# A first stage in a written-out order on all engines, its norm row spread by TensorE, its first tokens and row requested from two queues

## The chip, the cores and the metric

One core of a Trainium2 chip runs the whole kernel. The metric is device time in microseconds, from the start of the program to its end, as the median of several executions. One execution was also taken by the profiler. TensorE is called PE here (its weight loads PEld), VectorE DVE, ScalarE ACT, GpSimd POOL and SyncE SP.

## What is computed

The reference is a trunk of two layers on 512 tokens of 1024 features, in float32. In each layer:

- h = x / rms(x) * g_pre, for each token over its 1024 features;
- proj = h @ w_in, cut into queries, keys, values, gates and the inputs of the two branches below;
- a sparse attention branch (compressed, selected and window keys) and a gated linear attention branch;
- y = m_nsa * (o_nsa @ w_up_nsa) + m_gla * (o_gla @ w_up_gla), and out = y @ w_out;
- x = x + rms_norm(out) * g_post.

The stage that the change rewrites is the start of the first layer: the norm of all tokens, the transposes that put features on partitions, and the first 296 columns of the projection (two groups of values, the attention gates and the 16 columns of the decay gate).

## The kernel before

Nearly all of the kernel's time goes to dense products on PE. To keep float32 accuracy, each operand of a projection is split in two: a high part H (a copy rounded to a shorter mantissa, made by ACT) and a low part Lo (the difference, made by DVE). One product of reference is three on PE: high by high, high by low, low by high (`split3`, L158).

**The first stage.** The tokens lie in four tiles s = 0 to 3 of 128 tokens, each loaded as two halves of 512 features (`load_x`, L218). `load_rows` (L186) asks for the norm row g_pre as two transfers that write the same 2 KB half row to all 128 partitions. `norm_rows` (L192) squares one half on ACT (L196) and one on DVE (L197), adds the sums, takes the power -1/2 on POOL (L183) and scales both halves by it and by the norm row on DVE (L202). `to_hT` (L205) transposes eight 128x128 blocks on PE (L209), copies each half out of PSUM as high part on ACT (L212) and makes the low part on DVE (L213). The weights of these 296 columns come in three pieces A0, A1, A2 (three, three and two blocks of 128 features), each loaded into one of three `raw` buffers (L132) and split by ACT (L145) and DVE or, for A1, POOL (L146). `proj_A(s)` (L314) runs 8 times 3 products of 296 columns for tile s, and half way through it the transposes of tile s+1. Its result is read out at L322 to L324. The stage so has 96 products and 32 transposes on PE.

**What follows.** `proj_gv` (L328) runs 24 products of 512 columns for each tile; its weights gv0 to gv3 pass through the same three `raw` buffers, so that gv3 can be requested only when gv0 has been split. gv1 and gv2 reuse the split buffers of A0 and A1. Small operands (`wa_s`, `gaT`, L361 to L369) are prepared on ACT and DVE in the same stretch. Then come long runs of projections (`fm`, L164), put out piece by piece by `fill` between the steps of the attention. There each pair of score blocks makes a round trip through DRAM (L783, L786), and PE multiplies what comes back (L841).

**Order.** PE's order is the program's (`manual_schedule` for PE, L224). The other engines' instructions are put in order by a planner that works with modelled costs. Each engine then runs its instructions strictly in that order, and so does the queue of SP, which issues every transfer. The constant masks are made on POOL and DVE (`masks`, L231), interleaved by the planner with the first stage.

## Time and profile before

| | us |
|---|---|
| median of 3 runs | 818.92 |
| lowest and highest run | 813.81, 818.93 |
| the profiled execution, whole | 817.14 |
| its span, first to last instruction | 815.1 |
| PE busy in the span | 787.2 (97%) |
| DVE busy | 553.8 (68%) |
| ACT busy | 353.5 (43%) |
| POOL busy | 99.9 (12%) |

The profiled execution lies 1.78 us below the median of the runs and 3.33 us above the lowest. What the profile does not show of it (817.14 less 815.1) is 2.04 us around the span. Times in the rows below count from the span's start. "Busy" is the time in which an engine had an instruction under way; matmuls are pipelined, so their durations overlap, and their rate is read from the distance of their starts.

### The profile page before, as it was taken

To read this page: it belongs to the slowest core of one execution; us is meant where nothing else is said; L and a number is where in the kernel's file an instruction comes from. 1 tells how busy PE (TensorE), PEld (TensorE's weight loads), DVE (VectorE), ACT (ScalarE), POOL (GpSimd) and SP (SyncE) were. 2 spreads that over 40 slices of the span, in tenths; PEclk is the share of its full clock that TensorE was granted. 3 is DMA by queue.
4 is the path that set the end of the run, shared out by engine and by line. 5 is a ranking of instruction groups with operands and counts; after the bars stand their busy time and mean duration, and the time that the engine had idled before them with its cause. 6 is when DMAs were issued, how large, how long until landed. Compare 5 with 4: busy or idle time off the path is not lost. (4 is left out here: it accounts for less than half of the span.)

```text
span 815.1 us, 12017 instructions
## 1 busy us (share of the span) xinstructions
PE 787.2 (97%) x4250; PEld 646.6 (79%) x4250; DVE 553.8 (68%) x1272; ACT 353.5 (43%) x727; POOL 99.9 (12%) x118
## 2 busy tenths in 40 slices
PE   3999999999989999999999999999999999999996
PEld 3888788888868787888888878888878788788885
DVE  5653848899987963655574457599999988266323
ACT  4591136555443533543246513456545544244211
POOL 3100024000000102121010101321000101022100
PEclk9999999999999999999999999999999999999999
DMA  8442124358486674556246112244666676655222
GB/s 296 140 147 78 52 59 137 95 175 247 154 245 208 191 235 127 171 157 218 78 143 220 53 52 79 78 116 129 211 201 217 209 231 200 192 155 157 77 104 77
DMA packets 54555, 124.55 MB, mean 153 GB/s; under 512 B 6592, under 2 KB 23520, under 8 KB 54496
## 3 DMA queue, kind: packets, MB, share of 16 engines
q1 hardware_dynamic: 54496, 123.79, 49.2%
q8 instruction: 33, 0.54, 0.3%
q14 instruction: 26, 0.21, 0.1%
HBM read 95.46 MB, written 25.17 MB: 148 GB/s over the span
## 5 line engine op out<-in xcount | busy, mean ns | idle before, releaser
L160 PE MATMUL ps_mm<-hT,hl 128*128 128x512 f32 x544 | 217.5, 400 | 0.0
L161 PE MATMUL ps_mm<-hT,hl 128*128 128x512 f32 x544 | 212.4, 390 | 0.0
L162 PE MATMUL ps_mm<-hT,hl 128*128 128x512 f32 x544 | 212.1, 390 | 0.0
L145 ACT CAST hl<-raw 128x1024 fp32r<-128x1024 f32 (+3 forms) x110 | 100.2, 913 | 147.0 <-PE ps_mm L161 102.2
L146 DVE TENSOR_TENSOR hl<-raw,hl 128x1024 fp32r<-128x1024 f32 (+3 forms) x109 | 119.2, 1095 | 51.2 <-ACT hl L145 46.0
L160 PEld LDWEIGHTS ps_mm<-hT,hl 128*128 128x128 f32 x544 | 102.3, 188 | 23.2 <-issue 3.1
L162 PEld LDWEIGHTS ps_mm<-hT,hl 128*128 128x128 f32 x544 | 102.2, 188 | 22.2
L161 PEld LDWEIGHTS ps_mm<-hT,hl 128*128 128x128 f32 x544 | 102.5, 188 | 19.0
L815 ACT ACTIVATE g<-g,sx 128x128 f32<-128x128 f32 (+3 forms) x128 | 70.9, 555 | 68.2 <-DVE sx L813 67.6
L778 DVE STREAM_TRANSPOSE T<-g 128x256 f32<-128x256 f32 (+3 forms) x128 | 58.6, 490 | 0.7
L818 DVE TENSOR_SCALAR g<-g,sx,gt 128x128 f32<-128x128 f32 (+3 forms) x128 | 57.1, 459 | 1.5
L161 PE MATMUL ps_mm<-oT,hl 128*128 128x512 f32 x128 | 50.5, 394 | 1.7 <-POOL oT L849 1.7
L160 PE MATMUL ps_mm<-oT,hl 128*128 128x512 f32 x128 | 51.2, 400 | 0.0
L162 PE MATMUL ps_mm<-oT,hl 128*128 128x512 f32 x128 | 50.1, 391 | 0.0
L841 PE MATMUL ps_o<-PT,a 128*64 128x256 f32 (+1 forms) x384 | 39.8, 353 | 4.6 <-DMA PT<-tp 4.6
L849 POOL TENSOR_TENSOR oT<-p,oT 128x512 fp32r<-128x512 f32 x8 | 13.9, 1738 | 241.7 <-ACT oT L848 241.7
L841 PEld LDWEIGHTS ps_o<-PT,a 128*64 128x64 f32 x384 | 26.1, 138 | 19.2 <-issue 10.2
L183 POOL TENSOR_TENSOR rs<-ms,mhalf 128x1 f32<-128x1 f32 (+1 forms) x24 | 18.0, 751 | 175.1 <-DVE ms L181 170.5
L869 POOL TENSOR_TENSOR p<-p,g 128x512 f32<-128x512 f32 x16 | 28.0, 1751 | 84.2 <-DVE p L868 78.5
L162 PE MATMUL ps_mm<-hl,hT 128*128 128x296 f32 (+1 forms) x96 | 32.7, 341 | 1.4 <-DVE hT L213 1.4
L160 PE MATMUL ps_mm<-hl,hT 128*128 128x296 f32 (+1 forms) x96 | 33.1, 345 | 0.7 <-ACT hT L212 0.7
L161 PE MATMUL ps_mm<-hl,hT 128*128 128x296 f32 (+1 forms) x96 | 32.5, 338 | 0.0
(253 smaller groups left out, 1310.1 us busy)
## 6 DMA issues: line engine op xcount, KB each, us to landing
raw<-wpk SPq DMA_DIRECT2D x96, 512.0 KB, 3.8
tp<-T SPq DMA_DIRECT2D x16, 896.0 KB, 4.4
PT<-tp SPq DMA_DIRECT2D x64, 224.0 KB, 4.9
raw<-wpk SPq DMA_DIRECT2D x32, 256.0 KB, 2.9
tp<-T SPq DMA_DIRECT2D x16, 384.0 KB, 2.8
PT<-tp SPq DMA_DIRECT2D x64, 96.0 KB, 2.4
a<-wpk SPq DMA_DIRECT2D x16, 256.0 KB, 4.3
p<-x SPq DMA_DIRECT2D x16, 256.0 KB, 2.9
```

Of the source, the lines that this page charges most:

```text
L145: A.copy(H[:, :w], r[:, :w])
L146: (G if i == 1 else V).tensor_tensor(Lo[:, :w], r[:, :w], H[:, :w].bitcast(F32), op=OP.subtract)
L160: mm(o, w[0], h[0], start=first, stop=False)
L161: mm(o, w[0], h[1], start=False, stop=False)
L162: mm(o, w[1], h[0], start=False, stop=last)
L183: G.tensor_tensor(r[:, :n], ms[:, :n], mhalf[:, :n], op=OP.pow)
L778: V.transpose(t[:, :, :, g], pps[g][:, :n * 128].rearrange("p (j b q) -> p b j q", j=n, b=4))
L815: A.activation(pp[:, :w], pp[:, :w], AF.Exp, bias=sx[:, 0:1], scale=-1.0, accum_out=sx[:, 1:2])
L818: V.tensor_scalar(pp[:, :w], pp[:, :w], sx[:, 2:3], gt[:, i, h * 3 + 1 + br:h * 3 + 2 + br], op0=OP.mult, op1=OP.mult)
L841: mm(acc[g * 64:(g + 1) * 64, (i0 + 2) * 128 - w:(i0 + 2) * 128], vsw[j // 2][:, j % 2, c0:c0 + 64], m, start=False, stop=(br == 1 and j = ...
L849: G.tensor_tensor(Lo, f_, H.bitcast(F32), op=OP.subtract)
L869: G.tensor_tensor(t_, t_, y2[f], op=OP.add)
```

## The change

The first stage of layer 0 becomes one function, `first_stage`, in which the order of ACT, DVE, POOL and SP is the program's as well.

- The second half of the first token tile and the norm row are requested from ACT's queue, the rest from SP's. The norm row is loaded as two half rows onto one partition of a zeroed tile, and two float32 matmuls with a matrix of ones write it to all partitions, in PSUM, where DVE reads it. The two broadcast transfers are gone in layer 0; the request for `spt` comes behind all tokens.
- PE runs 4 dummy matmuls of 512 columns ahead of that, 1 before and 2 after the first transposes, and 1 later (`keep_busy`).
- The products of a tile are regrouped by weight piece and part (`prod`): those with the high part of a weight first, those with its low part later, and transposes of the next tiles between them. Four tiles accumulate in PSUM side by side. The squares of tiles 2 and 3 are made by ACT alone. The low part of A1 is made by DVE.
- POOL draws all mask shapes at the start (`mask_shapes`); DVE's copies of them come behind the low part of A2 and ahead of the low part of the last tile.
- The ACT and DVE work for gv0 to gv3 and for `wa_s` and `gaT` is ordered behind the last tile's high and low parts (`behind_tokens`). It ties no transfer.
- Layer 1 keeps its code; `norm_rows` and `to_hT` are cut into helpers with the same instructions.

```diff
+
+
+WARM = (4, 1, 2)
...
         dma(r[:, :w], src)
+        if i < 3:
+            ready[l, n] = (new("hl", (128, 1024), F32R), new("hl", (128, 1024), F32R))
+            first_w.append((r, w) + ready[l, n])
+            return
...
         H, Lo = new("hl", (128, 1024), F32R), new("hl", (128, 1024), F32R)
         A.copy(H[:, :w], r[:, :w])
-        (G if i == 1 else V).tensor_tensor(Lo[:, :w], r[:, :w], H[:, :w].bitcast(F32), op=OP.subtract)
+        V.tensor_tensor(Lo[:, :w], r[:, :w], H[:, :w].bitcast(F32), op=OP.subtract)
         ready[l, n] = (H, Lo)
+    @contextmanager
+    def behind_tokens():
+
+        with ExitStack() as order:
+            for e in behind:
+                order.enter_context(tc.issue_after(e))
+            yield
 
     def issue(i):
         while issued[0] <= min(i, len(SEQ) - 1):
-            load(issued[0])
+            with behind_tokens() if issued[0] < 7 else nullcontext():
+                load(issued[0])
...
+    def square(q2, xh, xn, h, e):
+
+        if e is A:
+            A.activation(xn[h], xh[h], AF.Square, accum_out=q2[:, h:h + 1])
+        else:
+            V.scalar_tensor_tensor(xn[h], xh[h], 1.0, xh[h], op0=OP.mult, op1=OP.mult, accum_out=q2[:, h:h + 1])
+
+    def row_scale(q2):
         qs = new("sm", (128, 1), tag="qs")
         V.tensor_add(qs, q2[:, 0:1], q2[:, 1:2])
-        rs = rsqrt_mean(qs, 1, D)
+        return rsqrt_mean(qs, 1, D)
+
+    def scale_rows(xh, xn, rs, gpre):
         for h in range(2):
             V.scalar_tensor_tensor(xn[h], xh[h], rs[:, 0:1], gpre[h], op0=OP.mult, op1=OP.mult)
...
+    def turn_half(xn, h):
+        b = ps("t")
+        for j in range(4):
+            tp(b[:, j * 128:(j + 1) * 128], xn[h][:, j * 128:(j + 1) * 128], ident)
+        return b.rearrange("p (j n) -> p j n", j=4)
+
+    def high(s, h, b4, HT):
+        return A.copy(HT[0][h][:, :, s * 128:(s + 1) * 128], b4)
+
+    def low(s, h, b4, HT):
+        sl = slice(s * 128, (s + 1) * 128)
+        return V.tensor_sub(HT[1][h][:, :, sl], b4, HT[0][h][:, :, sl].bitcast(F32))
...
-        G.affine_select(out=tmp[:, 384:512], in_=tmp[:, 384:512], compare_op=OP.is_ge, fill=-NEG, base=0,
+    all_but_pe = tc.manual_schedule(engines={mybir.EngineType.Activation, mybir.EngineType.DVE,
+                                             mybir.EngineType.Pool, mybir.EngineType.SP})
+
+    def mask_shapes():
+
+        t = [new("g") for _ in range(2)]
+        G.memset(t[0], 0.0)
+        G.affine_select(out=t[0][:, 384:512], in_=t[0][:, 384:512], compare_op=OP.is_ge, fill=-NEG, base=0,
                         pattern=[[-1, 128]], channel_multiplier=1)
...
-        pmask = const((128, 4, 2, 32), BF, "pmask")
-        t4 = tmp[:, 0:256].rearrange("p (i g j) -> p i g j", i=4, g=2)
+        t4 = t[1][:, 0:256].rearrange("p (i g j) -> p i g j", i=4, g=2)
+        G.memset(t[1][:, 0:256], 0.0)
         G.affine_select(out=t4, in_=t4, compare_op=OP.is_ge, fill=-NEG, base=-31,
                         pattern=[[128, 4], [0, 2], [-16, 32]], channel_multiplier=1)
-        V.tensor_copy(pmask, t4)
...
         G.memset(hidv, 0.0)
+        return t[0], t4, valid, gmask, kbd, hidk, hidv
+
+    def masks(tmp, t4, valid, gmask, kbd, hidk, hidv):
+        ident_b = const((128, 128), BF, "ident_b")
+        V.tensor_copy(ident_b, ident)
+        cmask = const((128, 512), BF, "cmask")
+        V.tensor_copy(cmask, tmp)
+        pmask = const((128, 4, 2, 32), BF, "pmask")
+        V.tensor_copy(pmask, t4)
+        zero = new("g")[:, 0:128]
+        V.memset(zero, 0.0)
+        vbd = [const((128, 128), F32R, f"vbd{i}") for i in range(2)]
+        for t in vbd:
+            V.tensor_copy(t, zero)
         cst = const((128, 2, 512), F32, "cst")
...
         spt = new("const", (128, SP_TOT), tag="spt")
-        dma(spt, sp[l])
+        if l:
+            dma(spt, sp[l])
...
+        def first_stage():
+
+
+            ones, rows = new("p", dt=BF), [new("p") for _ in range(2)]
+            onef = new("p")[:, 0:128]
+            for t in rows:
+                V.memset(t, 0.0)
+            V.memset(ones, 1.0)
+            V.memset(onef, 1.0)
+            idle = ps("o")
+
+            def keep_busy(n):
+                for _ in range(n):
+                    mm(idle, ones[:, 0:128], ones, start=True, stop=True)
+
+            xs = [[new("g") for _ in range(2)]]
+            dma(xs[0][0], x[0:128, 0:512])
+            nc.scalar.dma_start(xs[0][1], x[0:128, 512:1024])
+            issue(0)
+            for h in range(2):
+                nc.scalar.dma_start(rows[h][0:1], gvec[0, 0:1, h * 512:(h + 1) * 512])
+            for i in range(3):
+                issue(i)
+                xs.append(load_x(x, i + 1, "g"))
+            dma(spt, sp[0])
+            shapes = mask_shapes()
+            keep_busy(WARM[0])
+            gpre = [ps("s") for _ in range(2)]
+            for h in range(2):
+                mm(gpre[h], onef, rows[h], start=True, stop=True)
+            xn = [[new("p") for _ in range(2)] for _ in range(2)]
+            q2 = [new("sm", (128, 2), tag="q2") for _ in range(4)]
+            xn += xn
+
+            def split_w(n, part):
+                r, w, H, Lo = first_w[n]
+                if part:
+                    V.tensor_sub(Lo[:, :w], r[:, :w], H[:, :w].bitcast(F32))
+                else:
+                    A.copy(H[:, :w], r[:, :w])
+
+            acc = [ps("mm") for _ in range(3)]
+
+            def prod(s, n, parts):
+
+                for part in parts:
+                    for k in range(n * 3, min(n * 3 + 3, KT)):
+                        w = first_w[n][2 + part][:, (k % 3) * 296:(k % 3) * 296 + 296]
+                        for t in hTs(k, s)[:2 - part]:
+                            mm(acc[s][:, :296], t, w, start=(s, k, 0) not in begun and k == 0 and part == 0,
+                               stop=(n == 2 and k == KT - 1 and part == 1))
+                            begun.add((s, k, 0))
+
+            begun = set()
+            square(q2[0], xs[0], xn[0], 0, A)
+            square(q2[0], xs[0], xn[0], 1, V)
+            rs = row_scale(q2[0])
+            split_w(0, 0)
+            square(q2[1], xs[1], xn[1], 0, A)
+            scale_rows(xs[0], xn[0], rs, gpre)
+            keep_busy(WARM[1])
+            b0 = [turn_half(xn[0], h) for h in range(2)]
+            keep_busy(WARM[2])
+            for h in range(2):
+                high(0, h, b0[h], HT)
+            square(q2[1], xs[1], xn[1], 1, V)
+            rs = row_scale(q2[1])
+            for h in range(2):
+                low(0, h, b0[h], HT)
+            split_w(1, 0)
+            scale_rows(xs[1], xn[1], rs, gpre)
+            prod(0, 0, (0,))
+            prod(0, 1, (0,))
+            b1 = [turn_half(xn[1], h) for h in range(2)]
+            square(q2[2], xs[2], xn[2], 0, A)
+            square(q2[2], xs[2], xn[2], 1, A)
+            split_w(2, 0)
+            split_w(0, 1)
+            rs = row_scale(q2[2])
+            for h in range(2):
+                high(1, h, b1[h], HT)
+                low(1, h, b1[h], HT)
+            keep_busy(1)
+            prod(0, 2, (0,))
+            prod(0, 0, (1,))
+            scale_rows(xs[2], xn[2], rs, gpre)
+            for n in range(3):
+                prod(1, n, (0,))
+            prod(1, 0, (1,))
+            b2 = [turn_half(xn[2], h) for h in range(2)]
+            square(q2[3], xs[3], xn[3], 0, A)
+            square(q2[3], xs[3], xn[3], 1, A)
+            split_w(1, 1)
+            rs = row_scale(q2[3])
+            for h in range(2):
+                high(2, h, b2[h], HT)
+                low(2, h, b2[h], HT)
+            prod(0, 1, (1,))
+            prod(1, 1, (1,))
+            scale_rows(xs[3], xn[3], rs, gpre)
+            split_w(2, 1)
+            drawn = masks(*shapes)
+            for n in range(3):
+                prod(2, n, (0,))
+            for n in range(2):
+                prod(2, n, (1,))
+            b3 = [turn_half(xn[3], h) for h in range(2)]
+            for h in range(2):
+                a = high(3, h, b3[h], HT)
+                v = low(3, h, b3[h], HT)
+            behind.extend((a.ins, v.ins))
+            for s in range(3):
+                prod(s, 2, (1,))
+                take_A(s, acc[s])
+            acc.append(ps("o"))
+            for n in range(3):
+                prod(3, n, (0, 1))
+            take_A(3, acc[3])
+            return drawn
+
         if l == 0:
-            to_hT(0, xn, HT)
-            issue(POS[0, "A1"])
-            xn1 = norm_rows(load_x(x, 1, "g"), gpre)
-            issue(POS[0, "A2"])
-            for s in range(ST):
-                if s + 1 < ST:
-                    xn = xn1 if s == 0 else norm_rows(load_x(x, s + 1, "g"), gpre)
-                    proj_A(s, lambda: to_hT(s + 1, xn, HT))
-                else:
-                    proj_A(s)
-            ident_b, cmask, pmask, valid, gmask, kbd, vbd, hidk, hidv, cos, sin = masks()
+            with all_but_pe:
+                ident_b, cmask, pmask, valid, gmask, kbd, vbd, hidk, hidv, cos, sin = first_stage()
         else:
             issue(POS[l, "A2"])
             for s in range(ST):
@@ -362,11 +518,12 @@
         zz = new("p")
         G.memset(zz, 0.0)
         dma(wa_f[0:16, 0:256], wa[l])
-        A.copy(gaT[0:96], zz[0:96])
-        A.copy(wa_s[0:96, 0:256], zz[0:96, 0:256])
-        A.copy(wa_s[0:16, 0:256], wa_f[0:16, 0:256])
-        A.copy(wa_s[64:80, 0:256], wa_f[0:16, 0:256])
-        V.tensor_sub(wa_s[32:48, 0:256], wa_f[0:16, 0:256], wa_s[0:16, 0:256].bitcast(F32))
+        with behind_tokens() if l == 0 else nullcontext():
+            A.copy(gaT[0:96], zz[0:96])
+            A.copy(wa_s[0:96, 0:256], zz[0:96, 0:256])
+            A.copy(wa_s[0:16, 0:256], wa_f[0:16, 0:256])
+            A.copy(wa_s[64:80, 0:256], wa_f[0:16, 0:256])
+            V.tensor_sub(wa_s[32:48, 0:256], wa_f[0:16, 0:256], wa_s[0:16, 0:256].bitcast(F32))
         rmask = new("p")
         G.memset(rmask, 1.0)
         G.memset(rmask[:, 0:512:64], 0.0)
```

## Rows read from the trace of the kernel before

**Rows 1.** PE's waits over the span: us in total, times, longest us.

```profile
PE ps_t L209 <- DVE p L202: 11.3, 3, 10.3
PE ps_o L841 <- DMA PT<-tp: 4.6, 3, 2.7
```

**Rows 2.** Windows: stretch, its length, busy time by engine, PEclk, DMA share, GB/s.

```profile
0.00:20.00 20.00, 7.69 (x30) 6.73 (x31) 10.94 (x23) 8.14 (x16) 6.72 (x22) 1.00 0.84 301
40.00:60.00 20.00, 20.00 (x92) 16.51 (x91) 11.03 (x16) 18.28 (x27) 0.99 (x2) 1.00 0.46 162
```

**Rows 3.** Timeline, chain to the unbroken products: start us, us, engine, line, operation.

```profile
2.18 0.91 SPq L189 DMA_DIRECT2D p<-gvec  x2
...
4.47 0.69 DVE L197 SCALAR_TENSOR_TENSOR p<-g 128x512 f32<-128x512 f32 x1 [4.47 <-DMA g<-x]
5.78 0.56 POOL L183 TENSOR_TENSOR rs<-ms,mhalf 128x1 f32<-128x1 f32 x1 [4.22 <-DVE ms L181]
8.47 1.08 DVE L146 TENSOR_TENSOR hl<-raw,hl 128x888 fp32r<-128x888 f32 x1 [2.85 <-ACT hl L145]
9.47 1.41 DVE L202 SCALAR_TENSOR_TENSOR p<-g,rs,p 128x512 f32<-128x512 f32 x2
...
12.17 2.31 DVE L197 SCALAR_TENSOR_TENSOR p<-g 128x512 f32<-128x512 f32 x1 [1.15 <-DMA g<-x]
15.14 0.61 PE L162 MATMUL ps_mm<-hl,hT 128*128 128x296 f32 x1 [1.36 <-DVE hT L213]
```

**Rows 4.** Timeline, PE alone, products and transposes at its two rates.

```profile
15.55 0.45 PE L160 MATMUL ps_mm<-hl,hT 128*128 128x296 f32 x1
17.53 0.45 PE L162 MATMUL ps_mm<-hl,hT 128*128 128x296 f32 x1
17.85 1.94 PE L209 MATMUL ps_t<-ident,p 128*128 128x128 f32 x8
21.07 0.34 PE L160 MATMUL ps_mm<-hl,hT 128*128 128x296 f32 x1
28.67 1.03 PE L209 MATMUL ps_t<-ident,p 128*128 128x128 f32 x8
29.82 0.30 PE L162 MATMUL ps_mm<-hl,hT 128*128 128x296 f32 x1
34.31 0.30 PE L162 MATMUL ps_mm<-hl,hT 128*128 128x296 f32 x1
34.45 0.40 PE L160 MATMUL ps_mm<-oT,hT 128*128 128x512 f32 x1
38.57 0.39 PE L160 MATMUL ps_mm<-oT,hT 128*128 128x512 f32 x1
```

**Rows 5.** Transfers issued from 0 to 18 us: KB each, median us to landing.

```profile
p<-gvec SPq DMA_DIRECT2D x2, 256.0 KB, 6.8
```

**Rows 6.** The small load of wa (L364): us from issue to landing.

```profile
DMA to landing us min/median/max: 1.7/2.1/2.5
```

**Rows 7.** Timeline, plain float32 matmuls of 128 columns, at the high rate.

```profile
107.00 2.05 PE L681 MATMUL ps_t<-g,p 128*128 128x128 f32 x16
```

**Rows 8.** DVE by line, 6.4 to 35 us: busy us, mean ns, idle before.

```profile
L202 DVE SCALAR_TENSOR_TENSOR p<-g,rs,p 128x512 f32<-128x512 f32 x8 | 5.9, 767 | 1.3 <-POOL rs L183 1.3
L213 DVE TENSOR_TENSOR hT<-ps_t,hT 128x512 fp32r<-128x512 f32 x8 | 5.3, 683 | 0.2 <-ACT hT L212 0.2
L239 DVE CAST cmask<-g 128x512 bf16<-128x512 f32 x1 | 0.4, 421 | 0.0
```

**Rows 9.** Timeline, load and split of gv3.

```profile
30.26 0.34 SPq L132 DMA_DIRECT2D raw<-wpk  x1
...
34.13 0.62 ACT L139 CAST oT<-raw 128x512 fp32r<-128x512 f32 x1 [0.60 <-DMA raw<-wpk]
```

**Rows 10.** Timeline of PE in the attention: its longest wait there.

```profile
238.76 2.48 PE L841 MATMUL ps_o<-PT,a 128*64 128x256 f32 x16 [2.74 <-DMA PT<-tp]
```

**Rows 11.** Windows of PE behind that wait: PE busy, PEclk, DMA share, GB/s.

```profile
239.00:244.00 5.00, 5.00 (x25) 0.66 0.63 207
```

More of the change, by code (lines that the diff above doesn't have):

```diff
@@ L1 @@
-from contextlib import ExitStack, nullcontext
+from contextlib import ExitStack, contextmanager, nullcontext
 import numpy as np
@@ L119, in trunk @@
     issued = [0]
+    first_w, behind = [], []
     def load(i):
```

39 lines of the change are left out of this document (11 added, 28 removed).

## The prediction

> **What bounds the kernel now.** I read the windows of 20 us first: PE has work in all of 40 to 60 us, but in only 7.69 of the first 20 [rows 2]. So PE bounds the body, and what the start loses is lost to the end. Then PE's waits: the longest in total stands at the start, 10.3 us before the first transpose; the next is 4.6 us for transfers in the attention [rows 1]. Then the timeline of the start, to see what each step waited for. The second half of the first tokens is there at 4.47 and the power that scales them ends at 5.78 + 0.56 = 6.34, but DVE scales only at 9.47: it stands behind A0's low part, which itself waited 2.85 us for ACT [rows 3]. The two broadcast requests of the norm row land 6.8 us after issue [rows 5], so they were hardly earlier. PE transposes at 10.28 and has unbroken work only from 15.14, because the low part of the tokens came late; before it DVE needed 2.31 us for a square of 0.69 us [rows 3].
>
> Last, PE's rate. Eight starts of products from 15.55 to 17.53 lie 0.2475 us apart, 33 starts from 29.82 to 34.31 lie 0.136 us apart; eight transposes take 1.94 us early and 1.03 late [rows 4]. The first is 296 columns at the 1.2 GHz level, the second nearly at 2.4. The rate changed at 21.07, after 5.9 us of unbroken work. (PEclk reads 1.00 there too [rows 2], so the distances are the better witness.) The stage ends at 34.45, where the first product of gv starts [rows 4].
>
> The sum goes against the profiled execution, 817.14 us. That is 1.78 below the median of the runs and 3.33 above the lowest. One per cent of the median, 8.2 us, is about what can be told from no change: under 810.7 is faster, over 827.1 slower.
>
> **The change, part by part.**
>
> *Scaling right after the power.* The order now puts DVE's scaling ahead of the weights' low parts, so it can start at 6.4 if the norm row is there: up to 3.1 us earlier than 9.47.
>
> *The norm row.* Two broadcasts go; two requests of one 2 KB row each come, issued on ACT's queue behind a half of x. Two issues took 0.91 us on SP [rows 3]; I give each of the three on ACT the same 0.45, an estimate, so the last leaves at about 2.1. Landing is bounded below by the small load, 1.7 us [rows 6], and above by the broadcasts, 6.8 [rows 5]: 3.8 to 8.9. I take 4.8, near the half of x that stands in the same queue and used to land at 4.47 [rows 3]. ACT's issuing is hidden: until x lands it has only its table load. Then the two float32 matmuls. Sixteen records of 128 columns take 2.05 us [rows 7], and the eight matmuls of that group leave two records each; 512 columns so cost 4 x 2 x 0.128 = 1.03 us at the high rate and, by 0.2475 / 0.136 = 1.82, 1.9 at the low. At the low rate the halves are ready at 6.8 and 8.7. DVE scales the second by 9.4 instead of 10.88.
>
> *Two queues.* In the first 20 us the transfers fill 0.84 of the engines' time at 301 GB/s [rows 2], so a second queue brings a request forward by its 0.45 us of issue, not bytes. Below, nothing; above, 0.45 for the second half of x; I take nothing, since the bytes set its landing. That 512 KB of broadcast no longer stand ahead of A1 and the later tokens I count as cover for the other steps, not as gain.
>
> *From scaled tokens to unbroken products.* After 9.4 DVE squares (0.69), adds and prepares (0.3), waits for ACT's high part, and makes the first low part (0.68 [rows 8]): about 11.5. Transposes of the second half (half of 1.94) lie beside it. So unbroken work starts at 11.5 instead of 15.14.
>
> *The rest of the stage on PE.* 95 products x 0.136, 24 transposes x 0.129 and a dummy: 12.9 + 3.1 + 0.2 = 16.2 us at the high rate. DVE has as much: 7 low parts x 0.68, 6 scalings x 0.75, three weight low parts of about 1.08, 1.08 and 0.7 (the first is in [rows 3], the last scaled by its width), mask copies about 1.4 (0.42 for the widest, L239, an estimate from its width), sums 0.9: 14.4, then 1.7 of PE work behind the last low part. DVE's list and PE's are so nearly equal that I add 0.5 for waits between them: 28.2, if the rate is high from 11.5.
>
> *The dummies* cost PE nothing: before the norm row and beside ACT's copies it is idle anyway. What they are worth is the moment of the higher rate; each us at the low rate costs 1 - 0.136/0.2475 = 0.45. Best is no loss. If the rise comes as long after the start of unbroken work as before, 5.9 us, it stands at 17.4 and 2.7 are lost. I take a rise at 13, nearer the first, since by the steps above the row's matmuls and the dummies give PE work from 4.8 on with gaps under a microsecond: 0.7. The stage ends at 28.9, against 34.45: **5.5 us**.
>
> Transposes I count at the rate of the products around them: eight took 0.243 us each early and 0.129 each late [rows 4]. The Trainium skill ("TensorE: Matmul & The Clock Gate", "Part 4: PE-mode transpose") says otherwise: the full rate does not engage for them. By that rule the 24 would cost 0.243 each and the sum would be 814.3. The trace disagrees with it.
>
> *Moved work.* POOL's masks now run ahead of the power, while tokens are in flight. POOL worked 6.72 us in the first 20 [rows 2], the powers and A1's low part among it, so the masks are less; all of it from 0.8 on would end at 7.5 and hold the power 1.7 us. I take nothing, for the power was wanted at 5.78 [rows 3]. `spt` is first used behind gv. A1's low part moves from POOL to DVE: it is in DVE's list above, and it takes POOL off the stretch of the 2.31 us square.
>
> *The new wait.* Splitting gv0 now stands behind the last tile's low part, about 26.4, and behind it on ACT stand gv1, gv2 and the small operands; gv3 is requested when gv0 is split. Two halves of 0.69 us: 27.8. It used to take 34.13 - 30.26 = 3.87 to land [rows 9]: 31.7, split in about 1.3. PE wants it 38.57 - 34.45 = 4.12 after the stage's end [rows 4]: 33.0. So it is just in time. Bounds: nothing, or 2.3 us if ACT runs the result copies and small operands first. I take nothing. gv2 can be requested only when A2's low part is made, which the new order puts behind the last scaling, at about 22 by DVE's list; 3.87 later it is there, still ahead of its turn. The queue of SP holds nothing else then but `cst` and later weights.
>
> Sum: 817.14 - 5.5 = **811.6**.
>
> **Rivals.**
>
> *A later stall goes.* In the attention PE waits 2.74 us for what comes back from DRAM [rows 10], and behind that wait the granted clock is 0.66 over 5 us [rows 11], part of it at the 1.2 GHz level, which costs 0.34 x 5 = 1.7 more. A shift of 5 us in the start changes which weight transfers this round trip meets. If the stall goes: 817.14 - 5.5 - 4.4 = 807.2. For it: the lowest run of before lies 5.1 us under the other two, near that price. Against it: nothing in the change touches that round trip.
>
> *The row comes late, or the rate does.* Row at the upper bound, 8.9: the stage moves by up to 4.1, ends at 33.0, 815.7. Rate at 17.4: 30.9, 813.6.
>
> *gv3 late:* 2.3 more, 813.9.
>
> *Transposes stay at the low rate* while products run at the high one: 24 x (0.243 - 0.129) = 2.7 more, 814.3. It is the mechanism of the rule above; the late row of 1.03 us for eight speaks against it [rows 4].
>
> *Slower than before: the rate stays low.* The new order cuts PE's work into shorter runs with transposes and waits between. If that keeps PE at 1.2 GHz through the stage, 119 pieces x 0.2475 = 29.5 from 11.5 end at 41.0, and 817.14 + 6.5 = 823.7. At 0.45 a us it turns to a loss when the rate rises later than (34.45 - 28.2) / 0.45 = 13.9 us after 11.5, at 25.4. Against it: the stretch before the rise at 21.07 had eight transposes in it too [rows 4].
>
> *The change does not do what it says:* the planner still orders all that lies outside the function. It cannot put gv's splits ahead of the last tokens, so this is the rival of gv3.
>
> **How the numbers follow.** Forecast, 28 to 30 us for the end of the stage and the rest unchanged: 0.50, 810.7 to 813. Later stall gone: 0.20. Row or rate late: 0.16. Transposes slow: 0.02. gv3: 0.07. Rate low throughout: 0.05. The range goes from 806.5 to 816.5; it takes in all but the last and the edges, about what two runs in ten may add by the spread of before. Faster by over 1%: the 0.20, and 0.14 of the forecast where the stage ends at or under 28 or a run falls low, 0.34. Slower by over 1% needs the last rival and more: 0.03. Within 1%: 0.63.
>
> **What would show it.** Right: first scaling at 6.4 to 7, unbroken products from 11 to 12 us, products 0.136 apart from about 13, the first product of gv at 28 to 30, no wait of PE for gv3. Wrong: the row's matmuls starting after 7; products 0.2475 apart past 17; DVE idle for POOL before the first scaling; a wait for `oT` at the seventh block of gv. If the stage ends at 29 and the time does not fall by 5, the difference lies in the attention's waits and granted clock.

## The result and the profile after

| | before, same chip | after |
|---|---|---|
| median of 7 runs | 816.2 us | 811.07 us |
| lowest and highest | 813.81, 818.93 | 808.68, 812.32 |
| profiled execution, its span | 817.14, 815.1 | 808.68, 807.0 |
| PE busy in the span | 787.2 (97%) | 789.5 (98%) |

The ratio of the times is 0.9918 [0.9900, 0.9936]: faster by 0.8%, 5.1 us between the medians, where 811.6 was forecast. That lies inside the 1% that the prediction counts as no change. The profiled execution of after is the lowest of its seven, so its 8.46 us against that of before are more than the change is worth. They lie here: 6.43 up to the first product of gv, 0.69 given back in the 24 products behind it, 2.36 in the rest of the span and 0.36 around it.

The window that answers to [rows 2], in its columns; PE is busy 17.05 us of the first 20, where it was 7.69:

```profile
0.00:20.00 20.00, 17.05 (x82) 11.82 (x83) 13.56 (x30) 10.75 (x22) 6.82 (x30) 1.00 0.67 232
```

The timeline of after, the chain to the unbroken products, which answers to [rows 3]:

```profile
0.80 0.41 ACTq L403 DMA_DIRECT2D g<-x  x1
...
1.49 0.77 ACTq L406 DMA_DIRECT2D p<-gvec  x2
...
4.39 0.69 DVE L214 SCALAR_TENSOR_TENSOR p<-g 128x512 f32<-128x512 f32 x1 [1.70 <-DMA g<-x]
...
4.65 4.11 PE L415 MATMUL ps_s<-p,p 128*128 128x512 f32 x4 [0.16 <-DMA p<-gvec]
...
5.63 0.57 POOL L200 TENSOR_TENSOR rs<-ms,mhalf 128x1 f32<-128x1 f32 x1 [1.36 <-DVE ms L198]
...
6.81 0.75 DVE L223 SCALAR_TENSOR_TENSOR p<-g,rs,ps_s 128x512 f32<-128x512 f32 x1 [1.26 <-PE ps_s L415]
...
8.80 0.75 DVE L223 SCALAR_TENSOR_TENSOR p<-g,rs,ps_s 128x512 f32<-128x512 f32 x1 [1.24 <-PE ps_s L415]
...
11.44 1.84 PE L435 MATMUL ps_mm<-hl,hT 128*128 128x296 f32 x11 [0.18 <-DVE hT L245]
```

The power ends at 6.20. Each half is scaled when PE has written its half of the row: the chain now goes through the row's matmuls, not through A0's low part. Unbroken work starts at 11.44 instead of 15.14.

PE alone in after, which answers to [rows 4] and shows the gv stretch. The rate rises inside the first tile's eight transposes: they start 0.213 us apart up to 10.26 and 0.11 apart behind 10.42, 1.71 us in all. Eleven products in 1.84 and the next eight transposes in 1.03 are at the high rate already, where before the rate changed at 21.07:

```profile
8.98 1.71 PE L237 MATMUL ps_t<-ident,p 128*128 128x128 f32 x8
...
13.12 1.03 PE L237 MATMUL ps_t<-ident,p 128*128 128x128 f32 x8
...
28.02 0.39 PE L177 MATMUL ps_mm<-oT,hT 128*128 128x512 f32 x1
28.25 0.39 PE L178 MATMUL ps_mm<-oT,hT 128*128 128x512 f32 x1
...
30.91 0.40 PE L177 MATMUL ps_mm<-hl,hT 128*128 128x512 f32 x1
31.47 0.50 PE L178 MATMUL ps_mm<-hl,hT 128*128 128x512 f32 x1 [0.16 <-DVE hl L154]
...
32.97 0.46 PE L178 MATMUL ps_mm<-oT,hT 128*128 128x512 f32 x1
33.27 0.39 PE L179 MATMUL ps_mm<-oT,hT 128*128 128x512 f32 x1
34.19 0.60 PE L533 MATMUL ps_t<-ident,ga 128*16 128x128 f32 x4
```

Products of 512 columns start 0.23 us apart (28.02, 28.25); 30.91 to 31.47 is 0.56, 31.47 to 31.81 and 29.65 to 29.99 are 0.34 each, and 32.97 to 33.27 is 0.30. From the first of them to the transposes of `ga` (the next work on PE) it is 6.17 us, 5.48 before (34.45 to 39.93). ACT shows what stands ahead of these weights. Its gv splits (L147, L153) stand between the small operands (L522 to L524) and the results of proj_A:

```profile
24.38 0.63 ACT L147 CAST oT<-raw 128x512 fp32r<-128x512 f32 x1
24.90 0.62 ACT L522 CAST p<-p 96x512 fp32r<-96x512 f32 x1
25.42 0.41 ACT L523 CAST p<-p 96x256 fp32r<-96x256 f32 x1
...
26.73 0.66 ACT L147 CAST oT<-raw 128x512 fp32r<-128x512 f32 x1
27.25 1.09 ACT L153 CAST hl<-raw 128x1024 fp32r<-128x1024 f32 x1
28.20 0.40 ACT L524 CAST p<-p 16x256 fp32r<-16x256 f32 x1
```

In the attention the waits for what comes back from DRAM are still there, 3.9 us for 4.6 [rows 1], but the granted clock reads 1.00 behind them, where it was 0.66 [rows 11]. The wait that answers to [rows 10], and the windows of PE around it:

```profile
232.29 1.74 PE L998 MATMUL ps_o<-PT,a 128*64 128x256 f32 x16 [2.06 <-DMA PT<-tp]
```

```profile
232.00:238.00 6.00, 5.71 (x34) 4.60 (x35) 5.72 (x14) 2.44 (x6) 1.17 (x1) 1.00 0.61 216
```

### The profile page after: what moved, and what is told of

The parts are those of the page before. It is cut to its first block, busy times and chain, and to the rows that moved or that the text cites. A ratio compares the mean times of both kernels' runs of the same rounds, so it can differ in the third digit from the quotient of the medians.

```text
span 807.0 us, 12043 instructions
## 1 busy us (share of the span) xinstructions
PE 789.5 (98%) x4262; PEld 644.4 (80%) x4262; DVE 553.5 (69%) x1274; ACT 354.4 (44%) x731; POOL 97.6 (12%) x117
## 5 line engine op out<-in xcount | busy, mean ns | idle before, releaser
L153 ACT CAST hl<-raw 128x1024 fp32r<-128x1024 f32 (+3 forms) x107 | 97.6, 915 | 138.3 <-PE ps_mm L178 99.9
L154 DVE TENSOR_TENSOR hl<-raw,hl 128x1024 fp32r<-128x1024 f32 (+3 forms) x107 | 117.4, 1098 | 47.6 <-ACT hl L153 42.5
L1006 POOL TENSOR_TENSOR oT<-p,oT 128x512 fp32r<-128x512 f32 x8 | 14.3, 1784 | 239.0 <-ACT oT L1005 239.0
L970 DVE CUSTOM_DVE_ANT_0 g<-ps_t,cmask 128x256 f32<-128x256 f32 (+3 forms) x64 | 28.8, 477 | 2.3 <-PE ps_t L957 2.2
L970 DVE CUSTOM_DVE_ANT_0 g<-ps_s,cmask 128x128 f32<-128x128 f32 (+3 forms) x64 | 29.0, 481 | 1.7 <-PE ps_s L957 1.7
L178 PEld LDWEIGHTS ps_mm<-oT,hl 128*128 128x128 f32 x128 | 24.1, 188 | 6.5 <-POOL oT L1006 2.3
```

The costliest lines, as they stand in the source:

```text
L153: A.copy(H[:, :w], r[:, :w])
L154: V.tensor_tensor(Lo[:, :w], r[:, :w], H[:, :w].bitcast(F32), op=OP.subtract)
L178: mm(o, w[0], h[1], start=False, stop=False)
L970: V.tensor_tensor_reduce(pp[:, :w], ob, cmask[:, 512 - w:512], 1.0, -3 * NEG, OP.add, OP.min, sx[:, 0:1])
```

## The experiments

One account holds for every profiled execution. Beside the start (to the `ga` transposes) two things differ: how long PE waits for the round trips in the attention, and in how many of the two stretches with such waits (220 to 260 and 620 to 640 us) the clock falls, which the 20 us window then shows as 0.91 or 0.92. A fall costs (1 - 0.91) x 20 = 1.8 or (1 - 0.92) x 20 = 1.6, about 1.7 us, as 0.34 x 5 did in [rows 11]. Span = 807.0 + (`ga` - 34.19) + 1.7 x falls + (waits - 3.9) gives every span to within 0.5 us:

| kernel | first gv product | `ga` | falls | waits | account | span | median (runs), ratio [95%] |
|---|---|---|---|---|---|---|---|
| before | 34.45 | 39.93 | 1 | 4.6 | 815.1 | 815.1 | 816.2 (7) |
| after | 28.02 | 34.19 | 0 | 3.9 | – | 807.0 | 811.07 (7), 0.9918 [0.9900, 0.9936] |
| after_again | 26.62 | 32.85 | 1 | 6.4 | 809.9 | 809.7 | 809.57 (6), 0.9895 [0.9875, 0.9915] |
| e1_no_dummies | 27.70 | 34.03 | 1 | 4.9 | 809.5 | 809.3 | 811.24 (4), 0.9922 [0.9901, 0.9944] |
| e2_planner_order | 30.56 | 36.77 | 2 | 4.8 | 813.9 | 813.5 | 812.29 (7), 0.9943 [0.9922, 0.9965] |
| e3_broadcast_row | 28.82 | 34.96 | 2 | 4.1 | 811.4 | 811.1 | 810.68 (4), 0.9917 [0.9901, 0.9934] |
| e4_one_queue | 28.63 | 34.80 | 2 | 4.4 | 811.5 | 811.2 | 812.49 (4), 0.9943 [0.9928, 0.9958] |
| e5_row_alone | 31.55 | 37.02 | 1 | 4.1 | 811.7 | 811.3 | 812.88 (6), 0.9948 [0.9924, 0.9972] |
| e6_before_dummies | 33.79 | 39.26 | 1 | 4.0 | 813.9 | 813.5 | 817.32 (10), 1.0003 [0.9986, 1.0020] |
| e7_row_first | 29.66 | 35.78 | 1 | 4.3 | 810.7 | 810.5 | 812.07 (4), 0.9938 [0.9922, 0.9954] |
| e8_gv_first | 28.08 | 34.00 | 2 | 4.1 | 810.4 | 810.0 | 812.2 (4), 0.9940 [0.9918, 0.9962] |
| e10_row_on_sp | 28.50 | 34.63 | 2 | 4.9 | 811.8 | 811.4 | 810.72 (5), 0.9909 [0.9877, 0.9942] |
| e11_order_alone | 29.63 | 35.83 | 1 | 4.2 | 810.6 | 810.4 | 814.62 (10), 0.9971 [0.9953, 0.9990] |
| e13_best | 27.07 | 32.99 | 0 | 4.5 | 806.4 | 806.3 | 808.59 (6), 0.9885 [0.9864, 0.9905] |

The ratios are against the kernel before on the same chip: its medians were 816.92 (e1 to e4), 816.67 (e5 to e8), 817.2 (e10, e11) and 818.15 (e13, after_again). The start of a kernel is compared by its `ga` column, with one caution: the same kernel gave 34.19 and 32.85 (after, after_again), 1.34 us apart, and every other kernel has one profiled execution. So differences of the start from after of up to about 1.3 us (e1, e3, e4, e8, e10, e13) are not shown by it.

### after_again: the changed kernel once more

> The changed kernel unchanged, beside the best version on the same chip, and as a second look at its own profile: stage end again at 27.7 to 28.5 if the moment of the higher rate repeats (11.4 in the first look), up to 29.5 if it moves by 3 us. Time 0.990 to 0.994 of the kernel before.

PE of this execution, its start and its longest wait, and the window around the wait:

```profile
5.00 2.58 PE L415 MATMUL ps_s<-p,p 128*128 128x512 f32 x4 [0.51 <-DVE p L214]
...
10.09 1.76 PE L435 MATMUL ps_mm<-hl,hT 128*128 128x296 f32 x11 [0.44 <-DVE hT L245]
...
231.74 3.25 PE L998 MATMUL ps_o<-PT,a 128*64 128x256 f32 x16 [2.89 <-DMA PT<-tp]
```

```profile
230.00:236.00 6.00, 4.26 (x21) 2.81 (x22) 4.53 (x16) 1.62 (x5) 0.00 (x0) 0.72 0.75 269
```

The row's four records take 2.58 us, not 4.11: the high rate was granted inside them, and all behind is 1.3 to 1.4 us earlier. Later a wait of 2.89 us is followed by a clock of 0.72, sixteen products take 3.25 instead of 1.74, and the execution is longer all the same (811.53 for 808.68). A second such wait, 2.49 us before 629.30, leaves the clock at 1.00. The two executions are of one kernel, so neither difference is the change's doing.

### e1_no_dummies

```diff
-WARM = (4, 1, 2)
+WARM = (0, 0, 0)
...
-            keep_busy(1)
```

> The changed kernel without any dummy matmul (all of WARM at 0, and the later one gone). Stage end (first product of gv) is 34.45 us before and 28.02 in the changed kernel, whose products were already 0.14 us apart from 11.44. Theory (the dummies bring the higher rate forward): unbroken work starts at the same 11 to 12 us but at 0.2475 us a product, the rate rises at 13 to 17, the stage ends at 28.7 to 30.5, time 0.7 to 2.5 us above the changed kernel. Rival (the norm row's own float32 matmuls keep PE at work long enough, the dummies are worth nothing): rate high from the first products, stage ends at 27.7 to 28.2, time equal.

```profile
4.90 3.75 PE L415 MATMUL ps_s<-p,p 128*128 128x512 f32 x4 [4.90 <-DMA p<-gvec]
...
11.15 1.78 PE L435 MATMUL ps_mm<-hl,hT 128*128 128x296 f32 x11 [0.57 <-DVE hT L245]
```

The same time, and products at the high rate from 11.15. Beside the row's matmuls, which keep PE at work from 4.90, the dummies are worth nothing here that can be measured, as the rival had it.

### e2_planner_order: all but the written-out order

```diff
-    all_but_pe = tc.manual_schedule(engines={mybir.EngineType.Activation, mybir.EngineType.DVE,
-                                             mybir.EngineType.Pool, mybir.EngineType.SP})
+    all_but_pe = nullcontext()
```

> The changed kernel with the written-out order of ACT, DVE, POOL and SP undone in the first stage (the planner orders them again; PE's order, the row by TensorE, the two queues and the dummies stay). Here the planner puts the first tile's low parts behind the second tile's square and scaling, the masks behind the second power. Theory (the order is worth a good part): first low part at 12 to 13 instead of 10.7, later waits of PE for low parts, stage ends at 29.5 to 31.5, time 1.5 to 3.5 above the changed kernel. Rival (row and dummies did it all): stage ends at 28 to 28.5, time equal.

```profile
9.90 1.64 PE L237 MATMUL ps_t<-ident,p 128*128 128x128 f32 x8 [1.74 <-DVE p L223]
...
11.83 3.17 PE L434 MATMUL ps_mm<-hl,hT 128*128 128x296 f32 x12
```

```profile
10.50:13.00 2.50, 2.50 (x10) 1.72 (x10) 2.50 (x6) 2.41 (x7) 1.06 (x4) 0.55 0.99 381
```

DVE of the same kernel:

```profile
7.90 0.69 DVE L214 SCALAR_TENSOR_TENSOR p<-g 128x512 f32<-128x512 f32 x1 [2.39 <-DMA g<-x]
...
9.11 2.71 DVE L223 SCALAR_TENSOR_TENSOR p<-g,rs,ps_s 128x512 f32<-128x512 f32 x4
11.74 1.28 DVE L245 TENSOR_TENSOR hT<-ps_t,hT 128x512 fp32r<-128x512 f32 x2
```

The start loses 2.6 us, as the theory had it. The row comes as early (its matmuls start at 4.66), but DVE first waits for the next tile to square it, then scales, both tiles in one go, and only then makes the first low part. PE idles 1.74 us before the transposes and the clock reads 0.55 behind that.

### e11_order_alone: broadcast row, one queue, no dummies

```diff
-WARM = (4, 1, 2)
+WARM = (0, 0, 0)
...
-            nc.scalar.dma_start(xs[0][1], x[0:128, 512:1024])
+            dma(xs[0][1], x[0:128, 512:1024])
             issue(0)
-            for h in range(2):
-                nc.scalar.dma_start(rows[h][0:1], gvec[0, 0:1, h * 512:(h + 1) * 512])
+            gpre = load_rows(0, 0)
...
-            gpre = [ps("s") for _ in range(2)]
-            for h in range(2):
-                mm(gpre[h], onef, rows[h], start=True, stop=True)
...
-            keep_busy(1)
```

> The changed kernel with all but its order undone: norm row by the two broadcasts, all requests on SP's queue, no dummies; the written-out order, the regrouped products, the squares on ACT and the early masks stay. The row alone, in the order of before, ended the stage at 31.55 (2.9 of the 6.4 us), while taking the row out of the changed kernel cost only 0.8. Theory (both shorten the same start of the chain, so the order alone has most of it too): first scaling at 8.5 to 9.5, stage ends at 28.8 to 30, time 0.8 to 2.5 above the changed kernel. Rival (the parts add up, order 6.4 - 2.9 = 3.5): stage ends at 30.9 or later, time 3 or more above.

```profile
11.97 3.06 PE L427 MATMUL ps_mm<-hl,hT 128*128 128x296 f32 x11 [0.37 <-DVE hT L245]
14.85 1.05 PE L237 MATMUL ps_t<-ident,p 128*128 128x128 f32 x8
```

The order alone (with the regrouped products, the squares on ACT and the early masks) takes 4.1 us off the start (39.93 to 35.83). DVE still waits for the broadcast (its first scaling is at 8.38), and unbroken work starts only 0.5 us later than with the row; but PE had no work at all before 9.19, and eleven products take 3.06 us, 0.25 apart; the rate rises only with the transposes at 14.85. The stage ends as the theory had it, the time is the rival's. Its ratio lies 0.5% (4.3 us) above that of after, of which its start accounts for 1.6 (3.0 against after_again); its profiled execution (812.10) was the lowest of ten, so that no trace shows where the rest goes.

### e5_row_alone: the row's matmuls in the kernel before

```diff
-    gpre = load_rows(0, 0)
+    onef, rows = new("p")[:, 0:128], [new("p") for _ in range(2)]
+    V.memset(onef, 1.0)
+    gpre = [ps("s") for _ in range(2)]
+    for h in range(2):
+        V.memset(rows[h], 0.0)
+        dma(rows[h][0:1], gvec[0, 0:1, h * 512:(h + 1) * 512])
+        mm(gpre[h], onef, rows[h], start=True, stop=True)
```

> The kernel before with one part of the change alone: the norm row loaded as one 2 KB row and spread by the two float32 matmuls, all requests on SP's queue, the planner's order kept (A0's low part still ahead of the first scaling). Theory (order is worth more than the row; putting the broadcasts back in the changed kernel cost 0.8 us of stage): first scaling at 7.5 to 8.7 instead of 9.47, the DVE square beside POOL still long, stage ends at 32.5 to 34, time 0.5 to 2 below the kernel before. Rival (the row carries the gain): stage ends at 30 or earlier, time 4 or more below.

DVE and POOL, then PE:

```profile
10.01 2.06 POOL L146 TENSOR_TENSOR hl<-raw,hl 128x888 fp32r<-128x888 f32 x1 [2.73 <-ACT hl L145]
```

```profile
10.29 2.34 DVE L197 SCALAR_TENSOR_TENSOR p<-g 128x512 f32<-128x512 f32 x1 [1.33 <-DMA g<-x]
...
12.55 0.74 DVE L202 SCALAR_TENSOR_TENSOR p<-g,rs,ps_s 128x512 f32<-128x512 f32 x1
```

```profile
17.81 0.38 PE L160 MATMUL ps_mm<-hl,hT 128*128 128x296 f32 x1
18.03 0.30 PE L161 MATMUL ps_mm<-hl,hT 128*128 128x296 f32 x1
```

Stage end 31.55, between what the theory and its rival had said: both missed. The row was ready by 9.0, but the planner put the square of the next tile ahead of the second scaling, and that square took 2.34 us beside POOL's subtraction, as in [rows 3]: 12.55. The gain of 2.9 is in the rate, high from 17.8 instead of 21.07, besides unbroken work from 13.76 instead of 15.14.

The two parts alone take 4.1 and 2.9 us off the start; together the two executions of the change show 5.7 and 7.1. In time, the order gives 0.29% and the row 0.52%, against 0.82 and 1.05% together. Whether they overlap is inside that spread.

### e3_broadcast_row: order, dummies and two queues, without the row's matmuls

```diff
...
-            for h in range(2):
-                nc.scalar.dma_start(rows[h][0:1], gvec[0, 0:1, h * 512:(h + 1) * 512])
+            gpre = load_rows(0, 0)
...
-            gpre = [ps("s") for _ in range(2)]
-            for h in range(2):
-                mm(gpre[h], onef, rows[h], start=True, stop=True)
```

> The changed kernel with the norm row loaded by the two broadcast transfers again, on SP's queue behind A0 as before; the two row matmuls are left out, dummies and order stay. Theory (the row by TensorE gains little by itself, since its second half was ready only at 8.7): the broadcasts land at 7.5 to 9.4, the first scaling runs at 8 to 9.5 instead of 6.8, the second right behind, later tokens and A1 land about 1.3 us later; stage ends at 28.5 to 30.5, time 0.5 to 2.5 above. Rival (the row by TensorE is the main part): stage ends at 31 or later, time 3 or more above.

```profile
8.65 1.41 DVE L223 SCALAR_TENSOR_TENSOR p<-g,rs,p 128x512 f32<-128x512 f32 x2 [3.12 <-DMA p<-gvec]
```

The start is 0.8 later, within the spread, and the time the same. Here, without the row's matmuls, two dummies follow the transposes and the rate rises at about 12; e11, which has neither, has it at about 14.85. The first scaling comes 1.84 later than in after, but both halves go at once: with the row on PE the second half waits for the row's second matmul (1.24 us, at the low rate). So the last scaling ends at 10.06, 0.5 behind after's 9.55.

### e4_one_queue

```diff
-            nc.scalar.dma_start(xs[0][1], x[0:128, 512:1024])
+            dma(xs[0][1], x[0:128, 512:1024])
...
-                nc.scalar.dma_start(rows[h][0:1], gvec[0, 0:1, h * 512:(h + 1) * 512])
+                dma(rows[h][0:1], gvec[0, 0:1, h * 512:(h + 1) * 512])
```

> The changed kernel with the second half of the first tokens and the norm row requested from SP's queue like all else (half of x directly behind the first half, the row behind A0). Theory (a second queue brings a request forward, not bytes): x's second half lands as in the changed kernel within 0.4 us, the row behind A0's 444 KB about 1 us later than 4.6, stage ends at 28.0 to 29.2, time 0 to 1.2 above. Rival (two queues matter): x's second half or the row 2 us or more later, stage ends at 30 or later.

The second half of x is there at 4.26 (4.39 in after): the second queue brings it nothing. The row's matmuls start at 5.42 instead of 4.65, and the start ends 0.6 later: within the spread of the start, so the step at 5.42 is the better witness. By the ratios the time is 2.0 us above that of after, more than the 0 to 1.2 expected, with intervals that overlap; the profiled execution has two clock falls, after's none.

### e7_row_first: the row ahead of the half of x on ACT's queue, on one partition, no dummies

```diff
...
-            nc.scalar.dma_start(xs[0][1], x[0:128, 512:1024])
-            issue(0)
             for h in range(2):
                 nc.scalar.dma_start(rows[h][0:1], gvec[0, 0:1, h * 512:(h + 1) * 512])
+            nc.scalar.dma_start(xs[0][1], x[0:128, 512:1024])
+            issue(0)
...
-                mm(gpre[h], onef, rows[h], start=True, stop=True)
+                mm(gpre[h], onef[0:1], rows[h][0:1], start=True, stop=True)
...
```

> The changed kernel without dummies, its row requested first on ACT's queue (ahead of the half of x, without waiting for a zeroed tile) and spread by matmuls over one partition instead of 128. In the changed kernel the second scaling waited 1.24 us for the row's second matmul and ran at 8.80. Theory (that wait is on the chain): the row lands at about 2.7, both matmuls end by 6.8, scaling runs at 6.3 to 7.8, first low part 1 us earlier than 10.70, stage ends at 26.6 to 27.6, time 0.4 to 1.5 below the changed kernel. Rival (the chain is then held by ACT, which waits for A0 and squares the second tile, or by DVE's list): stage ends at 27.7 to 28.2, time equal. Slower: the half of x, requested 0.8 later, lands later by as much, stage 28.5.

```profile
1.58 0.41 ACTq L397 DMA_DIRECT2D g<-x  x1
...
2.21 3.75 PE L406 MATMUL ps_s<-p,p 1*128 1x512 f32 x4 [2.21 <-DMA p<-gvec]
...
7.29 0.69 DVE L214 SCALAR_TENSOR_TENSOR p<-g 128x512 f32<-128x512 f32 x1 [6.22 <-DMA g<-x]
```

The row's matmuls start 2.4 us earlier, and the start ends 1.6 later. The half of x was requested 0.78 later and landed 2.9 later (7.29 for 4.39). The Trainium skill ("DMA: Bandwidth & Descriptors", "Issuing engines are not separate DMA queues") says that issuing from several engines saves only the time of issuing, since all transfers interleave on the same engines. If the time of issuing were all, the loss would be 0.8, an estimate from the 0.78; the measurement is 2.9. A0's request, on SP at 1.24 in both, went out behind the half of x in after and ahead of it here; that this is what let the transfers of A0 and the next tokens in ahead is argued from the order of the requests. Two more runs agree: with the half of x requested ahead of A0 it is there at 4.26 (e4) and 3.45 (e10). No run changes that order alone. The time is 1.6 us above that of after by the ratios, with intervals that overlap.

### e10_row_on_sp: the row as SP's first request, on one partition, no dummies

```diff
...
+            dma(row[0:1].rearrange("p h n -> p (h n)"), gvec[0, 0:1])
             dma(xs[0][0], x[0:128, 0:512])
...
-            for h in range(2):
-                nc.scalar.dma_start(rows[h][0:1], gvec[0, 0:1, h * 512:(h + 1) * 512])
...
-                mm(gpre[h], onef, rows[h], start=True, stop=True)
+                mm(gpre[h], onef[0:1], row[0:1, h], start=True, stop=True)
...
```

> The changed kernel without dummies, the row one request of 4 KB, the first on SP's queue, spread by matmuls over one partition; the half of x is again the first request on ACT's queue, as in the changed kernel. With the row ahead of the half of x on ACT's queue, that half landed at 7.29 instead of 4.39, since A0 and the next tokens got ahead of it, and the stage ended at 29.66. Theory (place in the queues decides, and a row at hand by 2.5 takes the 1.24 us wait of the second scaling away): half of x by 4.8, power done by 6.4, scalings at 6.4 to 7.9, first low part at 9.7 to 10.2, stage ends at 26.7 to 27.6, time 0.5 to 1.3 below the changed kernel. Rival (ACT's wait for A0 and its square of the second tile then hold the first high part): first low part at 10.5 or later, stage ends at 27.6 to 28.3.

```profile
6.86 1.97 PE L237 MATMUL ps_t<-ident,p 128*128 128x128 f32 x8 [0.77 <-DVE p L223]
...
9.99 3.08 PE L425 MATMUL ps_mm<-hl,hT 128*128 128x296 f32 x11 [0.42 <-DVE hT L245]
12.87 1.91 PE L237 MATMUL ps_t<-ident,p 128*128 128x128 f32 x8
```

Row and half of x are both early (matmuls at 2.34, last scaling done at 7.46), and unbroken work starts 1.4 us earlier than in after. But it runs at the low rate until the second transposes are over, and the start ends at 34.63, no earlier. The row's matmuls are there as in e1, but PE idles behind them: 0.77 us before the first transposes and 0.42 before the unbroken products. An earlier chain bought more time at half the rate. Both expectations missed in part: the scalings came as the theory had them, the stage end (28.50) is later than either.

### e6_before_dummies: 22 dummies in the kernel before

```diff
+    ones, idle = new("const", (128, 512), BF, tag="ones"), ps("o")
+    V.memset(ones, 1.0)
+    for _ in range(22):
+        mm(idle, ones[:, 0:128], ones, start=True, stop=True)
```

> The kernel before with 22 dummy matmuls of 512 columns ahead of its first transposes (22 x 0.43 = 9.4 us of idle PE filled, ending at about 11), nothing else. It asks what the rate alone was worth: before, the products up to 21.07 ran at 0.2475 us. Theory (the rate is a third of the stage's gain): products 0.137 apart from the start, but PE then waits longer for tokens, since the chain on DVE and ACT is the same; stage ends at 31.5 to 33.5, time 1 to 3 below. Rival 1 (the chain alone set the stage): ends at 34 or later, time equal. Rival 2 (the rate was nearly all): ends at 30 or earlier.

```profile
1.52 6.23 PE L233 MATMUL ps_o<-ones 128*128 128x512 bf16 x22 [1.52 <-DVE ones L231]
...
14.44 0.62 PE L162 MATMUL ps_mm<-hl,hT 128*128 128x296 f32 x1 [1.36 <-DVE hT L213]
14.85 0.45 PE L160 MATMUL ps_mm<-hl,hT 128*128 128x296 f32 x1
```

```profile
12.00:21.00 9.00, 6.96 (x27) 6.27 (x28) 7.86 (x17) 4.26 (x10) 3.54 (x6) 0.50 0.79 309
```

No difference in time, as the first rival had it. The stage ends 0.66 us earlier, but so do the steps before it (transposes at 9.33 for 10.28, the third product at 14.44 for 15.14), so it is not the rate. Twenty-two dummies in 6.23 us are 0.28 each, where the four of after took 1.89, 0.47 each: the rate rose inside them. Then PE waited 1.58, 1.56 and 1.36 us between 7.75 and 14.44, and the products ran 0.2475 apart again until 21.2. A rate gained early is lost in waits; so this run does not say what the high rate alone would be worth with the old order.

### e8_gv_first: gv's splits ahead of the small operands on ACT

```diff
-                A.copy(H, rr)
-                V.tensor_sub(Lo, rr, H.bitcast(F32))
+                a = A.copy(H, rr)
+                v = V.tensor_sub(Lo, rr, H.bitcast(F32))
+                if i == 3 and h == 1:
+                    behind.extend((a.ins, v.ins))
...
+        if i == 5:
+            behind.extend((a.ins, v.ins))
```

> The changed kernel with the small operands (wa_s, gaT) ordered behind the splits of gv1 and gv2, and those behind gv0's. In the changed kernel 24 products of gv took 28.02 to 34.19, 6.17 us, against 5.48 before (34.45 to 39.93): 0.69 given back, with short waits for DVE's low part of gv1 and gv2. Theory (the splits stand behind 1.0 us of small copies on ACT): that stretch falls to 5.5 to 5.7, stage end unchanged at 28.0, time 0.4 to 0.7 below the changed kernel. Rival (DVE's own 1.2 us for each low part is the limit): 6.0 to 6.2, time equal.

```profile
32.28 0.39 PE L181 MATMUL ps_mm<-oT,hT 128*128 128x512 f32 x1
32.72 0.50 PE L182 MATMUL ps_mm<-oT,hT 128*128 128x512 f32 x1
```

The stretch from the first gv product to `ga` takes 5.92 instead of 6.17: a gain of 0.25, between the two expectations. The waits at gv1 and gv2 go down; one for gv3 takes their place (0.44 between 32.28 and 32.72, 0.23 is the pace). The time is no lower: by the ratios 1.8 us above that of after, with intervals that overlap and two clock falls in the profiled execution.

### e13_best: row on SP, three dummies ahead and two around the transposes, gv's splits first

```diff
-WARM = (4, 1, 2)
+WARM = (3, 2, 2)
...
+                if i == 3 and h == 1:
+                    behind.extend((a.ins, v.ins))
...
+            dma(row[0:1].rearrange("p h n -> p (h n)"), gvec[0, 0:1])
...
-                mm(gpre[h], onef, rows[h], start=True, stop=True)
+                mm(gpre[h], onef[0:1], row[0:1, h], start=True, stop=True)
...
-            keep_busy(1)
```

> The row as one first request on SP's queue spread over one partition (its scalings ran at 6.05 to 7.46 and unbroken products from 9.99, but at 0.25 us until about 14.4, and the stage ended at 28.50), with dummies back where PE idled there: 3 ahead of the row's matmuls, 2 behind them, 2 behind the first transposes; and gv1, gv2 and the small operands ordered behind gv0's split. Theory (with the chain shorter, the rate decides, and dummies keep PE's work unbroken from 1.5 on): rate high from about 10, stage ends at 26.6 to 27.5, gv's first 24 products take 5.9, time 0.6 to 1.5 below the changed kernel. Rival (dummies are worth nothing, as in the changed kernel, where leaving them out moved the stage by 0.3 the other way): low rate to about 14, stage ends at 28.3 or later, time equal.

```profile
10.03 2.36 PE L437 MATMUL ps_mm<-hl,hT 128*128 128x296 f32 x12
```

With the dummies the early chain has a higher rate than in e10: twelve products in 2.36, 0.135 apart from 10.87, where e10 has 0.247 until past 12.8. So, as far as one execution of each tells, dummies bring the rate forward where PE would idle behind the row's matmuls; the stage ends at 27.07 against 28.50, as the theory had it, and the start ends at 32.99. But after_again, on the same chip, is at 32.85, and the medians are 808.59 and 809.57 with intervals that overlap. Both beat the kernel before; that this version beats the change is not shown.

## Why the prediction was right

By the steps of the prediction:

| step | predicted | after |
|---|---|---|
| row lands, first matmul | 4.8 | 4.65 |
| scalings | 6.8; second done by 9.4 | 6.81; done at 9.55 |
| unbroken work | 11.5 | 11.44 |
| high rate from | 13 | about 10.4 |
| first product of gv | 28.9 | 28.02 |
| gv stretch | as before | + 0.69 |
| rest of the span | as before | - 2.36 |

- **The start held step by step.** Row, matmuls at the low rate, two scalings and the first low parts came within 0.2 us. Which part is worth what: the order, with all that e11 keeps beside it, 4.1 us on its own, the planner's order undone alone 2.6 (e2); the row 2.9 on its own (e5), and within the order 0.8 (e3), which lies inside the spread.
- **The rate term was mis-sized.** Taken as 0.7 (a rise at 13), it was the best case, nothing: the rate rose at about 10.4, ahead of the unbroken work, and eleven products from 11.44 take 1.84 us, where the low rate takes 3.06 (e11). From 11.44 to 28.02 are 16.6 us, 16.2 had been worked out for PE's work alone, so of the 0.5 for waits 0.4 was spent. Together the stage ended 0.9 us earlier than forecast, 0.7 of it the rate. The dummies were not needed for that moment: e1 has none and rises at about 9.5. But the row's matmuls alone do not set it either: e7 and e10 have them, idle behind them and rise at 14.3 to 15, like e11, which has neither; with dummies in those gaps e13 rises between 10.0 and 10.6. And the moment moves from one execution to the next (10.4 in after, between 6.0 and 6.6 in after_again), so these single executions show where the rate rose, not what fixes it.
- **Two queues counted at nothing** was right for x (4.26 on one queue, 4.39 on two) and wrong for the row, which comes 0.8 later on one (e4). What stood ahead of the half of x counted for more (e7, by 2.9 us), as far as the order of the requests explains it.
- **Masks and A1's low part at nothing:** right. POOL was done before the power's operand came: it waited 1.36 us for DVE at 5.63.
- **Transposes go with their surroundings:** right. Eight in 1.03 at 13.12, among products at the high rate, against 1.91 in e10 among products at the low one; in after the rate even rises inside the transposes at 8.98. The rule of the Trainium skill ("TensorE: Matmul & The Clock Gate", "Part 4: PE-mode transpose"), by which the full rate would not engage, does not hold here.
- **gv3 just in time:** right in place, with a different wait ahead of it. It was split at 31.53 and wanted at 32.74, at 0.07 us of loss. The rest of the 0.69 is gv1 and gv2, whose splits stood behind gv0's second half and the small operands on ACT. That this order costs it is shown for 0.25 (e8), the rest is argued. The bound of 2.3 held; the zero was too good.
- **The slower rival** needed a rise past 25; it came at about 10.4.
- **The later stall, rival of 0.20,** came in by half in the profiled execution and not by the change. The wait stayed (2.06 us for 2.74) and the clock's fall was absent; the same kernel in after_again has a wait of 2.89 and the fall. Between the medians 5.1 us remain; the start alone took 5.7 less in one execution and 7.1 less in the other.
- **Luck in the closeness.** Up to `ga` 5.5 us were forecast and 5.74 measured, but 0.9 gained in the stage and 0.69 lost behind it nearly cancel, and the second execution of the same kernel shows 7.08. That 811.6 lies 0.5 from the median of 811.07 owes something to the base as well: the sum started from 817.14, 0.94 above the median of before's seven runs.

Left open: why the order alone, e11, is slower than its start makes it; what the rate alone would have been worth before; whether order and row overlap.

## What to carry to other kernels

In a start that ends in a chain across engines, follow the chain to the first unbroken product of TensorE, and cost the rate it will have there beside the moment: e10 came 1.4 us earlier and ended no earlier. Useful small matmuls ahead (here the spread of a row) did what dummies were meant to do where the transposes followed them at once (e1), and did not where PE idled behind them (e7, e10). When executions of one kernel differ by several us, account for the late waits and clock falls first, then compare the stretch that the change touches.

## What the hardware showed that was not expected

- **The granted clock in the profile is not the rate before the first rise.** In e6, from 12 to 21 us, products are 0.2475 apart and PEclk reads 0.50. In the kernel before, the same products at the same distance read 1.00 in the same window:

```profile
12.00:21.00 9.00, 6.96 (x28) 6.16 (x27) 8.22 (x16) 4.46 (x11) 4.33 (x6) 1.00 0.86 326
```

- **The same kernel's rate rises at different moments.** After's row matmuls took 4.11 us in one execution and 2.58 in another; the `ga` transposes 34.19 and 32.85.
- **A late wait of PE may or may not cost the clock.** After a wait of 2.06 us it stayed at 1.00 (after), after 2.89 it read 0.72 over 6 us (after_again). The length of the wait does not decide it: after 1.96 us it fell (e8, before 627.98), after 2.49 it did not (after_again, before 629.30). Two such places in the kernel make 0 to 2 falls of about 1.7 us. The runs agree: the four of e1 had mean granted clocks of 0.999, 0.995, 0.995 and 0.993 and took 808.08, 811.04, 811.45 and 812.03 us.
- **A float32 matmul with one partition of data costs what one with 128 costs:** four records of 512 columns in 3.75 us in e7, e10 and e13 (one) and in e1, e4 and e5 (128).
